# One transformer block on one core: an earlier transpose in the hand-over to the feed forward, a sum on another engine, and one block product moved up

## The chip, the cores and the metric

The kernel runs on one core of one Trainium2 chip. The metric is the device time of one launch in microseconds (us). Times of before: a median of 1028.2 us over 3 runs, from 1026.87 to 1029.06.

Five engines matter. TensorE (PE) multiplies matrices into eight banks of PSUM, VectorE (DVE) and ScalarE (ACT) read these banks and work on SBUF, GpSimd (POOL) does small powers and issues DMAs that add to what lies in SBUF, and SyncE (SP) issues the weight loads.

## The reference

One block over 512 tokens of 1024 features, in float32: a gated input projection, a convolution branch, a state-space branch, an output projection with a residual, and a gated feed forward with a second residual. The change lies between the last two.

```python
mixed = (g_conv * conv_out + g_ssm * ssm_out) @ w_out[i]
x = x + rms_norm(mixed, mix_post_g[i])
h = rms_norm(x, ffn_pre_g[i])
gt, up = jnp.split(h @ w_gate_up[i], 2, axis=-1)
f = (jax.nn.silu(gt) * up) @ w_down[i]
x = x + rms_norm(f, ffn_post_g[i])
```

## The kernel before

**Precision.** Each float32 operand is split into a high and a low half of a shorter type, and each product is three matmuls (`mm3`: high with high, and the two mixed ones). "hi" and "lo" in the names are these halves. ACT rounds the high half, DVE subtracts it from the source for the low one. For some weights the low half is made by ACT (minus the high half) and an adding DMA from POOL's queue.

**Output projection.** Tokens come in four blocks t = 0 to 3 of 128. `tm_step(ps, t, k, ...)` does step k (of eight) of block t: two column halves of 512, three matmuls each, so six matmuls 512 wide. A list `steps` gives the order; the blocks 2 and 3 are done one after the other, k from 0 to 7. When a block's last step is done, `residual(t, ps)` reads its two banks: ACT squares them and sums, DVE multiplies them by the gain, POOL takes the power -1/2 in `factor`, DVE adds to the residual rows, and the same is done again for the second norm. What comes out is the new row block xr and a diagonal matrix dg of norm factors.

**Hand-over.** `transposed(t)` turns xr into feature-major order with 16 matmuls 128 wide against dg (tile ptr), which scales it too. DVE reads the first half of the result (xg0) and ACT the second (xg1), and both make the halves of the moving operands of the feed forward: b11 and b21 from even blocks; b22, t1, t2, t3, t4 once the odd block is there as well. `mark["hi"]` and `mark["lo"]` name the last halves issued. Blocks 2 and 3 make the second half of the tokens' columns, so that the first product of the feed forward, on b11, waits for block 2.

**Feed forward.** The up and gate projections are done in units u = 0 to 21 with a scheme that needs seven block products instead of eight: `first(u)` (two products, a11 with b11 into X[u] and a12 with b21 into Y[u]), `x2`, `v1`, `x3`, `v2`, `x4`. Each `product` is twelve matmuls 256 wide (four, times three). x2, x3 and x4 add on in X[u]: ACT copies X[u] out after `first` (noted c) and after x2, DVE adds it after x3 (noted x3), and x4 closes it. The order of the units 0 to 3 is written by hand (`start`); from unit 4 on it is first(u), x4(u-1), x2(u), v2(u-1), v1(u), x3(u).

The weights of a unit are prepared by `prep_a` (a11, a12) and `prep_s`: sums s1 = a21 + a22, s3 = a11 + a21, s2 = s1 + a11, s4 = s2 + a12, and their halves (`halve`). For the units in `ADD_S1`, s1 is made by two DMAs on POOL's queue, the second of which adds; otherwise by one DVE addition. Units 0 to 3 have their sums prepared early; unit 4's is in `ADD_S1`.

**What sets the order.** A planner orders each engine's instructions when the kernel is built, by the order in the source and its own costs. `not_before(a, b)` makes it place `a` behind `b` on an engine without a wait in the run; `tc.issue_after` does so for a group; `ORDER_DVE` and `ORDER_ACT` are chains of such edges over noted instructions (lo_s2_4 is the low half of s2 of unit 4). After the units' start `mark["chain"]` keeps all products in source order.

Of the kernel before, what the change touches and what calls it, by code (L numbers as in the profile page):

```python
# [22 lines left out]
NK = D // P  # L23
# [36 lines left out]
for _n, _c in PRM:  # L60
# [22 lines left out]
TAPS_GLU = 12  # L83
TAPS = (6, 14, 18, 20, 20, 20, 20, 20)
TAPS_GATE = 5
ADD_S1 = (3, 4, 5)
ORDER_DVE = (
# [3 lines left out]
).split()  # L91
ORDER_ACT = (
    "xg1 t1h t2h c0 b22h v1_0 t3h t4h hi_s2_1 x2_0 c1 hi_s3_1 v1_1 c2 c3 x2_1 hi_s2_2 hi_s1_2 si2_0 si3_0 hi_s3_2 hi_s2_4 c4 hi_s1_4 hi_s3_4 hi_s1_5"
# [47 lines left out]
def block_kernel(ctx: ExitStack, tc: tile.TileContext, x, xT, x0, prm, hp, gp, w, out):  # L141
# [12 lines left out]
    raws, split, more_raw = {}, {}, []  # L154
# [39 lines left out]
    mark = {}  # L194
# [6 lines left out]
    def not_before(ins, first):  # L201

        edge = mybir.DependencyInfo(mybir.DependencyClass.NoSync, mybir.DependencyReason.DATA)
        tc.add_manual_dep(ins.ins, first.ins.name, edge, reason="spread")

    def mm3(ps, lh, ll, rh, rl, start, stop, more=False):

        mark["pe"] = pe.matmul(ps, lh, rh, start=start, stop=False, skip_group_check=more)  # L208
        pe.matmul(ps, lh, rl, start=False, stop=False, skip_group_check=more)  # L209
        mark["pe3"] = pe.matmul(ps, ll, rh, start=False, stop=stop, skip_group_check=more)  # L210
        return mark["pe"]
# [78 lines left out]
    ps = aux_tile("warm_ps")  # L290
# [52 lines left out]
    for k in range(1, NK):  # L343
        sq = va_tile(f"sq{k}")
# [157 lines left out]
    for j in range(NK):  # L502
# [6 lines left out]
        if j == 0:  # L509
            three = [glu_tile(n) for n in ("pv0", "pg0", "pv1")]  # L510
            ws = [w_get("val", 0), w_get("glu", 0), w_get("val", 1)]
            for k in range(NK):
                for ps, (wh, wl) in zip(three, ws):
                    c = slice(k * P, (k + 1) * P)
# [451 lines left out]
    wo0 = seq[("wo", 0)]  # L966
# [75 lines left out]
    def tm_tiles(key):  # L1042
        return [[bank(f"tm_{key}_{t}_{n}") for n in range(2)] for t in range(NT)]

    def tm_step(ps, t, k, nk, ah, al, wt, ns=(0, 1)):

        wh, wl = wt
        for n in ns:
            c = slice(n * T, (n + 1) * T)
            mm3(ps[t][n], ah, al, wh[:, c], wl[:, c], k == 0, k == nk - 1)  # L1050

    def mean_sq(src, pool_, tag, n):
        ss = sm.tile([P, 1], F32, tag=f"ss{n}", bufs=2, name=f"ss{n}_{tag}")
# [134 lines left out]
    def residual(t, ps):  # L1188

        nonlocal hold  # L1190
        xr = pbp.tile([P, D], F32, tag="xr", name=f"xr{t}")
        nc.scalar.dma_start(xr, x[t * P : (t + 1) * P, :])
        mg = pbp.tile([P, D], F32, tag="mg", bufs=1, name=f"mg{t}")
        ss = []
        for n, c in enumerate(cols2):
            ss.append(mean_sq(ps[n], pbp, f"a{t}", n))
            m = dve.tensor_tensor(out=mg[:, c], in0=ps[n], in1=gpost0[:, c], op=ALU.mult)
        if t == 3:
            hold += [mark["sq"], m]
        rs = factor(ss, f"a{t}")  # L1200
        ss = []
        for n, c in enumerate(cols2):
            dve.scalar_tensor_tensor(out=xr[:, c], in0=mg[:, c], scalar=rs, in1=xr[:, c], op0=ALU.mult, op1=ALU.add)
            ss.append(mean_sq(xr[:, c], pbp, f"b{t}", n))
        rs = factor(ss, f"b{t}")
        dg = pbp.tile([P, P], F32, tag="dg", name=f"dg{t}")
        mark["dg"] = dve.tensor_scalar(out=dg, in0=ident, scalar1=rs, scalar2=None, op0=ALU.mult)
        mark[f"dg{t}"] = mark["dg"]
        xrs[t] = xr, dg
        nc.scalar.dma_start(x2d[t * P : (t + 1) * P, :], xr)  # L1210

    def transposed(t):

        tok = slice((t // 2) * P, (t // 2 + 1) * P)
        xr, dg = xrs[t]
        xg = []
        for n in range(2):
            pt = bank(f"ptr{t}_{n}", 2 * (t == 1) + n).rearrange("p (k q) -> p k q", k=KB)
            for k in range(KB):
                c = slice((KB * n + k) * P, (KB * n + k + 1) * P)  # L1220
                m = pe.matmul(pt[:, k, :], xr[:, c], dg, start=True, stop=True)
                if t >= 2:
                    not_before(m, mark["pe3"])
                    mark["pe3"] = m
            tg = dict(tag=f"xg{t}{n}", bufs=1) if t % 2 == 0 else dict(tag=f"xg{n}", bufs=1)
            xg.append(pmp.tile([P, KB, P], F32, name=f"xg{t}_{n}", **tg))
            if n == 0:
                note("xg0", dve.tensor_tensor(
                    out=xg[n], in0=pt, in1=b3(prm_t[:, FPG + KB * n : FPG + KB * n + KB], P), op=ALU.mult
                ))  # L1230
            else:
                for k in range(KB):
                    note("xg1", act.activation(
                        xg[n][:, k], pt[:, k], AF.Copy, scale=prm_t[:, FPG + KB + k : FPG + KB + k + 1]
                    ))

        def halved(name, src, sign=1.0):
            hi, lo = [m[:, :, tok] for m in mov[name]]
            if sign > 0:
                h_ = act.copy(hi, src)  # L1240
                l_ = dve.tensor_tensor(out=lo, in0=src, in1=hi.bitcast(F32), op=ALU.subtract)
            else:
                h_ = act.activation(hi, src, AF.Copy, scale=-1.0)
                l_ = dve.scalar_tensor_tensor(
                    out=lo, in0=src, scalar=-1.0, in1=hi.bitcast(F32), op0=ALU.mult, op1=ALU.subtract
                )
            if name == "b22":
                not_before(h_, mark["hi"])
                not_before(l_, mark["lo"])
            mark["hi"], mark["lo"] = mark[name] = note(name + "h", h_), note(name + "l", l_)  # L1250

        if t % 2 == 0:
            halved("b11", xg[0])
            halved("b21", xg[1])
            xgs[t] = xg
            return
        b11, b21 = xgs[t - 1]
        t1, t2 = [pmp.tile([P, KB, P], F32, tag=f"t{i}", bufs=1, name=f"t{i}_{t}") for i in (1, 2)]

        def sums():  # L1260
            note("t1", dve.tensor_tensor(out=t1, in0=b11, in1=xg[0], op=ALU.subtract))
            note("t2", dve.tensor_tensor(out=t2, in0=t1, in1=xg[1], op=ALU.add))
            halved("t1", t1)
            halved("t2", t2, -1.0)

        def rest():
            halved("b22", xg[1])
            note("t3", dve.tensor_tensor(out=t1, in0=xg[1], in1=xg[0], op=ALU.subtract))
            halved("t3", t1)
            note("t4", dve.tensor_tensor(out=t2, in0=t2, in1=b21, op=ALU.subtract))  # L1270
            halved("t4", t2)

        return sums, rest
# [4 lines left out]
    ps = tm_tiles("wo")  # L1278
    steps = [(t, k) for k in range(4) for t in (0, 1)] + [(t, k) for t in (0, 1) for k in range(4, NK)]
    steps += [(t, k) for t in (2, 3) for k in range(NK)]  # L1280
    for t, k in steps:
        (mh, ml), tok = mt[t // 2], slice(t % 2 * P, (t % 2 + 1) * P)
        tm_step(ps, t, k, NK, mh[:, k, tok], ml[:, k, tok], split[wo0 + k])
        if k == NK - 1:
            residual(t, ps[t])
            if t == 2:
                others()
        if (t, k) == (2, 1):
            transposed(0)
            first_room = [mp.tile([P, 2, 1024], F32R, tag=f"m0{p}", name=f"a01{p}") for p in "hl"]  # L1290
            for u in range(2):
                prep_a(u, [m[:, u] for m in first_room])
        if (t, k) == (2, 5):
            sums, others = transposed(1)
            sums()
        if (t, k) in ((3, 1), (3, 2)):
            prep_a(k + 1)
        if (t, k) == (3, 4):
            halves = prep_s(0)
        if (t, k) == (3, 5):  # L1300
            with tc.issue_after(mark["pe"].ins):
                transposed(2)

    sg = {}
    c1, c2 = slice(0, HB), slice(HB, T)
# [65 lines left out]
    def x3(u):  # L1371
        f, e = u // 2, u % 2
        d = D_[u][1][:, c2]
        product(X[u], u, "s3", "t3", False)
        note(f"x3_{u}", add(d, X[u]))
        if e == 0:
            note(f"si3_{u}", act.activation(d, d, AF.Silu, scale=-1.0))
        else:
            note(f"g3_{u}", gated_by(d, d, sg[f][1][:, c2]))
# [11 lines left out]
    def x4(u):  # L1391
        f, e = u // 2, u % 2
        d = D_[u][1][:, c1]
        product(X[u], u, "a22", "t4", False)
        if e == 0:
            act.activation(d, X[u], AF.Silu, scale=-1.0)
        else:
            note(f"g4_{u}", gated_by(d, X[u], sg[f][1][:, c1]))
# [94 lines left out]
    for u in range(NF):  # L1493
        last = u == NF - 1
        if u in start:
            for n in start[u].split():
                step[n[0]](int(n[1:]))
        else:
            first(u)
            if last:  # L1500
                prep(STEPS[1])
                prep(STEPS[2])
            x4(u - 1)
            x2(u)
            if last:
                prep(STEPS[3])
            v2(u - 1)
            v1(u)
            if last:
                prep(STEPS[4])  # L1510
            x3(u)
        prep_s(max(u + 1, 3))
        prep_a(max(u + 2, 4) if u else 3)
        if u == NF - 2:
            prep(STEPS[0])
# [188 lines left out]
```

## Time and profile before

| | before |
|---|---|
| timed runs, median of 3 | 1028.2 us (1026.87 to 1029.06) |
| the profiled execution's own time | 1023.46 us |
| its span, first to last instruction | 1021.7 us |
| PE busy | 1010.2 us (99%), 6181 matmuls |
| DVE busy | 842.3 us (82%) |
| ACT busy | 616.2 us (60%) |
| POOL busy | 107.3 us (11%) |

In lines of the order of time the first number is the start in us from the span's start, the second the duration; in brackets at the end stands how long the engine had idled and what released it. L12 is line 12 of the kernel before. Matmuls are pipelined: a line's duration is longer than the distance to the next one, and it is the distance that counts.

### The profile page before, as it was taken

To read this page: it belongs to the slowest core of one execution; us is meant where nothing else is said; L and a number is where in the kernel's file an instruction comes from. 1 tells how busy PE (TensorE), PEld (TensorE's weight loads), DVE (VectorE), ACT (ScalarE), POOL (GpSimd) and SP (SyncE) were. 2 spreads that over 40 slices of the span, in tenths; PEclk is the share of its full clock that TensorE was granted. 3 is DMA by queue.
4 is the path that set the end of the run, shared out by engine and by line. 5 is a ranking of instruction groups with operands and counts; after the bars stand their busy time and mean duration, and the time that the engine had idled before them with its cause. 6 is when DMAs were issued, how large, how long until landed. Compare 5 with 4: busy or idle time off the path is not lost. (4 is left out here: it accounts for less than half of the span.)

```text
span 1021.7 us, 15952 instructions
## 1 busy us (share of the span) xinstructions
PE 1010.2 (99%) x6181; PEld 882.4 (86%) x6181; DVE 842.3 (82%) x1226; ACT 616.2 (60%) x1034; POOL 107.3 (11%) x133
## 2 busy tenths in 40 slices
PE   9999999999999999999999999999999999999997
PEld 7898889888888888888888889889999999988885
DVE  7899977968595879588987789678899887799974
ACT  7655775667656656673452676466676565678542
POOL 0101102110121012101110110011100000002000
PEclk9999999999999999999999999999999999999999
DMA  8567635645464465456352465644756355469622
GB/s 299 151 161 226 158 94 144 186 108 163 142 163 116 120 179 148 112 153 150 79 144 70 117 187 124 227 109 119 227 146 196 113 152 159 124 190 296 195 83 82
DMA packets 44459, 156.07 MB, mean 153 GB/s; under 512 B 5152, under 2 KB 6176, under 8 KB 43360
## 3 DMA queue, kind: packets, MB, share of 16 engines
q1 hardware_dynamic: 30672, 104.66, 30.4%
q0 software_dynamic: 11504, 44.05, 22.0%
q10 hardware_dynamic: 2208, 6.36, 1.9%
q8 instruction: 48, 0.79, 0.3%
q14 instruction: 27, 0.22, 0.1%
HBM read 150.78 MB, written 4.26 MB: 152 GB/s over the span
## 5 line engine op out<-in xcount | busy, mean ns | idle before, releaser
L466 DVE SCALAR_TENSOR_TENSOR a<-v,prm_t,a 128x511 f32<-128x511 f32 (+15 forms) x240 | 180.7, 756 | 15.8 <-ACT a L463 13.8
L168 ACT CAST whi<-raw 128x1024 fp32r<-128x1024 f32 (+2 forms) x108 | 106.7, 1000 | 130.6 <-PE pso L209 37.5
L175 DVE TENSOR_TENSOR wlo<-raw,whi 128x1024 fp32r<-128x1024 f32 (+2 forms) x67 | 74.9, 1124 | 37.4 <-ACT whi L168 36.6
L173 POOL DMA_DIRECT2D wlo<-in_w x41 | 36.6, 892 | 377.3 <-ACT wlo L172 112.8
L209 PE MATMUL pz<-wlo,hhi 128*128 128x512 f32 (+2 forms) x160 | 56.2, 351 | 0.3 <-DVE wlo L175 0.3
L210 PE MATMUL pz<-whi,hlo 128*128 128x512 f32 (+2 forms) x160 | 56.3, 352 | 0.0
L208 PE MATMUL pz<-whi,hhi 128*128 128x512 f32 (+2 forms) x160 | 55.4, 353 | 0.0
L208 PE MATMUL px<-hhi,whi 128*128 128x512 f32 x128 | 50.2, 392 | 0.0
L208 PE MATMUL pso<-yh,whi 128*128 128x512 f32 x128 | 50.0, 393 | 0.0
L210 PE MATMUL px<-hhi,wlo 128*128 128x512 f32 x128 | 49.8, 389 | 0.0
L209 PE MATMUL px<-hlo,whi 128*128 128x512 f32 x128 | 49.8, 389 | 0.0
L209 PE MATMUL pso<-yl,whi 128*128 128x512 f32 x128 | 49.7, 390 | 0.0
L210 PE MATMUL pso<-yh,wlo 128*128 128x512 f32 x128 | 49.7, 389 | 0.0
L1119 ACT CAST whi_g<-raw 128x1024 fp32r<-128x1024 f32 x40 | 41.2, 1052 | 12.7 <-DVE raw L1158 7.4
L550 DVE SCALAR_TENSOR_TENSOR x<-px,prm_t,x 128x511 f32<-128x511 f32 (+2 forms) x48 | 34.7, 741 | 14.3 <-ACT x L548 14.3
L1124 DVE TENSOR_TENSOR wlo_g<-raw,whi_g 128x1024 fp32r<-128x1024 f32 x34 | 41.1, 1218 | 3.8 <-ACT whi_g L1119 3.7
L172 ACT ACTIVATE wlo<-whi 128x1024 fp32r<-128x1024 f32 x41 | 43.3, 1056 | 0.3
L448 ACT ACTIVATE L<-L,nacs 128x128 f32<-128x128 f32 x128 | 38.8, 389 | 0.1
L209 PEld LDWEIGHTS pz<-wlo,hhi 128*128 128x128 f32 x160 | 30.2, 188 | 4.7 <-DVE wlo L175 0.9
L208 PEld LDWEIGHTS pz<-whi,hhi 128*128 128x128 f32 x160 | 30.2, 188 | 3.9
L210 PEld LDWEIGHTS pz<-whi,hlo 128*128 128x128 f32 x160 | 30.2, 188 | 3.7
L1119 ACT CAST chi_g<-raw 128x1024 fp32r<-128x1024 f32 x24 | 24.9, 1055 | 12.5 <-DVE raw L1158 5.9
(749 smaller groups left out, 3442.6 us busy)
## 6 DMA issues: line engine op xcount, KB each, us to landing
raw<-in_w SPq DMA_DIRECT2D x182, 512.0 KB, 4.4
wlo<-in_w POOLq DMA_DIRECT2D x41, 512.0 KB, 6.6
L<-scr POOLq DMA_DIRECT2D x8, 1024.0 KB, 7.0
wlo_g<-in_w POOLq DMA_DIRECT2D x11, 512.0 KB, 6.6
clo_g<-in_w POOLq DMA_DIRECT2D x7, 512.0 KB, 5.6
pws<-in_w POOLq DMA_DIRECT2D x8, 256.0 KB, 6.0
pw_raws<-in_w SPq DMA_DIRECT2D x4, 512.0 KB, 6.3
xr<-in_x ACTq DMA_DIRECT2D x4, 512.0 KB, 4.2
```

The source lines that it names most:

```text
L168: act.copy(hi[:, c], src[:, c])
L172: act.activation(lo[:, c], hi[:, c].bitcast(F32), AF.Copy, scale=-1.0)
L173: mark["lo"] = pool.dma_start(lo[:, c], w[n][:, c].bitcast(F32R), accum_op=ALU.add)
L175: mark["wlo"] = dve.tensor_tensor(out=lo[:, c], in0=src[:, c], in1=hi[:, c].bitcast(F32), op=ALU.subtract)
L208: mark["pe"] = pe.matmul(ps, lh, rh, start=start, stop=False, skip_group_check=more)
L209: pe.matmul(ps, lh, rl, start=False, stop=False, skip_group_check=more)
L210: mark["pe3"] = pe.matmul(ps, ll, rh, start=False, stop=stop, skip_group_check=more)
L448: act.activation(L[:, h, c, :], L[:, h, c, :], AF.Exp, bias=nacs[:, c, HG * g + h : HG * g + h + 1])
L466: return dve.scalar_tensor_tensor(out=va[j][:, d:], in0=vs[j][:, : T - d], scalar=col("dw_w", j * KC + KC - 1 - d), in1=va[j][:, d:], op0= ...
L550: dve.scalar_tensor_tensor(out=a[:, d:], in0=ps[:, : T - d], scalar=col("ssm_w", i * KS + KS - 1 - d), in1=a[:, d:], op0=ALU.mult, op1=ALU ...
L1119: a_ = act.copy(hi, src)
L1124: d_ = dve.tensor_tensor(out=lo, in0=src, in1=hi.bitcast(F32), op=ALU.subtract)
```

## The change

Four edits. First, `transposed(2)` is called behind step (3,4) instead of (3,5), and step (3,5) gets an edge behind its last matmul (`behind=spread`). Second, in `residual(3)` ACT's squares are put behind `mark["hi"]` and DVE's products behind `mark["lo"]`, which are the halves of b21 of block 2 at that point. Third, unit 4 leaves `ADD_S1`: its s1 is one DVE addition, placed in `ORDER_DVE` ahead of s3_4. Fourth, x4(5) stands directly behind x3(5) instead of behind first(6) (`ROLL = 5`).

```diff
@@ -83,11 +83,12 @@
-ADD_S1 = (3, 4, 5)
+ROLL = 5
+ADD_S1 = (3, 5)
 ORDER_DVE = (
...
-    "s3_4 s2_4 v2_2 x3_3 s4_4 lo_s2_4 lo_s1_4 s3_5"
+    "s1_4 s3_4 s2_4 v2_2 x3_3 s4_4 lo_s2_4 lo_s1_4 s3_5"
 ).split()
@@ -1042,12 +1043,14 @@
-    def tm_step(ps, t, k, nk, ah, al, wt, ns=(0, 1)):
+    def tm_step(ps, t, k, nk, ah, al, wt, ns=(0, 1), behind=None):
 
         wh, wl = wt
         for n in ns:
             c = slice(n * T, (n + 1) * T)
-            mm3(ps[t][n], ah, al, wh[:, c], wl[:, c], k == 0, k == nk - 1)
+            m = mm3(ps[t][n], ah, al, wh[:, c], wl[:, c], k == 0, k == nk - 1)
+            if behind is not None:
+                not_before(m, behind)
@@ -1195,6 +1198,9 @@
             ss.append(mean_sq(ps[n], pbp, f"a{t}", n))
             m = dve.tensor_tensor(out=mg[:, c], in0=ps[n], in1=gpost0[:, c], op=ALU.mult)
+            if t == 3:
+                not_before(mark["sq"], mark["hi"])
+                not_before(m, mark["lo"])
@@ -1280,7 +1286,8 @@
-        tm_step(ps, t, k, NK, mh[:, k, tok], ml[:, k, tok], split[wo0 + k])
+        behind = spread if (t, k) == (3, 5) else None
+        tm_step(ps, t, k, NK, mh[:, k, tok], ml[:, k, tok], split[wo0 + k], behind=behind)
@@ -1297,9 +1304,9 @@
         if (t, k) == (3, 4):
             halves = prep_s(0)
-        if (t, k) == (3, 5):
             with tc.issue_after(mark["pe"].ins):
                 transposed(2)
+            spread = mark["pe3"]
@@ -1500,7 +1507,8 @@
-            x4(u - 1)
+            if u - 1 != ROLL:
+                x4(u - 1)
@@ -1509,6 +1517,8 @@
             x3(u)
+            if u == ROLL:
+                x4(u)
```

## The prediction

> **What bounds the kernel now.** I read the page first, then the list of TensorE's waits, then the order of time on each engine around the two places that the diff touches.
>
> ```profile
> span 1021.7 us, 15952 instructions
> PE 1010.2 (99%) x6181; PEld 882.4 (86%) x6181; DVE 842.3 (82%) x1226; ACT 616.2 (60%) x1034; POOL 107.3 (11%) x133
> PEclk9999999999999999999999999999999999999999
> ```
> ```profile
> PE yv L208 <- ACT f L1369: 1.0, 1, 1.0
> ```
>
> TensorE (PE) is busy for 1010.2 of 1021.7 us at a full clock, so an edit that neither adds nor removes a matmul can only move PE's waits. The diff does neither. The longest wait behind the output projection, quoted here, is 1.0 us, in the last unit of the feed forward; two in the hand-over and one in the fifth unit stand in the rows of parts A and B, 0.3 to 0.4 each. That is 2.1 us of idle time, and each costs a little more, because a waiting matmul comes late and the next one comes 0.11 later still. So what is to be had is small, and every new wait costs its full length.
>
> **Part A: the hand-over.** Transposes of block 2 move ahead of step (3,5) of the output projection, step (3,5) is put behind them, and the squares and products of block 3's residual are put behind the halves that the transposes feed.
>
> ```profile
> 677.82 0.39 PE L210 MATMUL tm_wo<-whi,m1l 128*128 128x512 f32 x1
> ...
> 683.94 0.39 PE L210 MATMUL tm_wo<-chi,m1l 128*128 128x512 f32 x1
> ...
> 687.34 0.39 PE L210 MATMUL tm_wo<-whi,m1l 128*128 128x512 f32 x1
> 687.57 1.95 PE L1221 MATMUL ptr<-dg,xr 128*128 128x128 f32 x16
> 689.27 0.48 PE L208 MATMUL tm_wo<-whi,m1h 128*128 128x512 f32 x1
> ...
> 690.05 0.38 PE L208 MATMUL xy<-b11h,a01h 128*128 128x256 f32 x1
> 690.78 0.39 PE L209 MATMUL xy<-b11l,a01h 128*128 128x256 f32 x1 [0.34 <-DVE b11l L1241]
> ...
> 693.00 0.38 PE L209 MATMUL xy<-b21l,a01h 128*128 128x256 f32 x1 [0.43 <-DVE b21l L1241]
> ...
> 700.06 1.95 PE L1221 MATMUL ptr<-dg,xr 128*128 128x128 f32 x16
> ```
> ```profile
> 685.22 0.29 DVE L1207 TENSOR_SCALAR dg<-ident,rs_b 128x128 f32<-128x128 f32 x1 [0.75 <-POOL rs_b L1063]
> ...
> 690.03 0.69 DVE L1241 TENSOR_TENSOR b11l<-xg,b11h 128x512 fp32r<-128x512 f32 x1
> ...
> 699.12 0.29 DVE L1207 TENSOR_SCALAR dg<-ident,rs_b 128x128 f32<-128x128 f32 x1 [0.44 <-POOL rs_b L1063]
> ```
>
> Matmuls 512 wide are 0.227 apart (42 from 677.82 to 687.34). The output projection does six for each step, so the row at 683.94 is the last of step (3,4) (three are left after the transposes, fifteen lie between), and today the transposes stand in the middle of step (3,7). In the new order they would be due at 683.94 + 0.23 = 684.17. They need the diagonal dg of block 2, which is complete at 685.22 + 0.29 = 685.51; a matmul starts 0.06 after the VectorE (DVE) work it waits for (b11l ends 690.72, matmul 690.78), so they start at 685.57. **New wait: 1.4 us.** Nothing covers it: PE has only (3,5) to (3,7) left before the transposes' results, and these are held behind them.
>
> After it, the transposes take 689.27 - 687.57 = 1.70, and eighteen matmuls take 18 x 0.227, with 0.1 for the first one's late start: first unit at 691.45, against 690.05 now.
>
> What goes: from 690.05 to 700.06 PE does 72 matmuls 256 wide. They need 8.16 to 8.47 us (0.1133 or 0.1177 each, see the table under cadence), so 1.5 to 1.8 us are waits on b11l and b21l. In the new order DVE and ScalarE (ACT) get the transposes' results 2 us earlier (685.57 instead of 687.57), so b21l, which ends at 692.95 today, is complete near 690.9 with no square in between, and PE asks for it after 691.45: both waits go. The second transposes are then due at 691.45 + 8.16 to 8.47 = 699.6 to 699.9, against 700.06.
>
> What is late next is block 3's diagonal, at 699.41 today. Its chain now starts 1.4 us later at the matmuls, but today its second square starts only at 690.92, behind four ACT scalings, and a product waits for it:
>
> ```profile
> 690.92 0.61 ACT L1055 ACTIVATE jk_a<-tm_wo 128x512 bf16<-128x512 f32 x1
> ```
>
> After the change the last projection matmul starts at 691.45 - 0.23 = 691.22 and ends 0.39 later, so that square starts at 691.6, 0.7 later; b21l's 0.6 on DVE, which lies between the products and the factor today, has gone. So the diagonal is ready at about 699.5, just before PE. **Part A: -0.3 us**, between -0.5 and +0.9 (if one more split of 1.2 us is planned into the chain).
>
> The longest wait of today, 1.0 us of idle time in the last unit, leaves the clock where it was (all slices of PEclk are at 9 or more); the new one is of that size. The Trainium skill ("TensorE: Matmul & The Clock Gate", "Why this matters for your kernels") says that PE drops to half its clock after about 3 us of idleness. By that rule a wait of 1.4 us costs no more than itself, and one twice as long would cost several us; no run here shows a gap that long.
>
> **Part B: the fifth unit's sum on DVE.** s1 of unit 4 was two accumulating DMAs on GpSimd's (POOL's) queue.
>
> ```profile
> 717.86 0.56 POOL L1149 DMA_DIRECT2D s<-in_w  x1 [11.84 <-DVE dlo L1124]
> 722.18 0.86 POOL L1150 DMA_DIRECT2D s<-in_w  x1 [3.76 <-DMA s<-in_w]
> ```
> ```profile
> 729.47 0.69 DVE L1157 TENSOR_TENSOR raw<-s,raw 128x512 f32<-128x512 f32 x1 [1.91 <-DMA s<-in_w]
> ...
> 732.60 1.23 DVE L1124 TENSOR_TENSOR clo_g<-raw,chi_g 128x1024 fp32r<-128x1024 f32 x1 [0.83 <-ACT chi_g L1119]
> ```
> ```profile
> 733.26 0.28 PE L209 MATMUL xy<-t2l,chi_g 128*128 128x256 f32 x1
> 733.88 0.38 PE L210 MATMUL xy<-t2h,clo_g 128*128 128x256 f32 x1 [0.35 <-DVE clo_g L1124]
> ```
>
> DVE idles 1.91 us for that DMA, then runs s2, s4 and the split on which PE waits: 733.88 - 733.26 - 0.11 = 0.51 late, and 0.11 for the next matmul, 0.62. The sum is 0.60 on DVE (two such sums follow each other at 749.25 and 749.85 below) and goes into the idle 1.91, so s2 comes 1.3 earlier and PE's wait of 0.5 goes. **Part B: -0.6 us**; at worst -0, if the idle time on DVE has been used up and the sum only delays what follows. The other queued DMA pair, unit 5's, no longer stands behind this one on POOL's queue, which can only bring it earlier.
>
> **Part C: the sixth unit.** Block product x4(5) accumulates into the same bank from which DVE adds x3(5), so it has to wait for that add. Today two products of unit 6 lie between.
>
> ```profile
> 749.16 0.28 PE L210 MATMUL xy<-t3h,wlo_g 128*128 128x256 f32 x1
> 749.28 0.28 PE L208 MATMUL xy<-b11h,whi_g 128*128 128x256 f32 x1
> ```
> ```profile
> 749.25 0.68 DVE L1152 TENSOR_TENSOR s<-raw 128x512 f32<-128x512 f32 x1
> 749.85 0.68 DVE L1157 TENSOR_TENSOR raw<-s,raw 128x512 f32<-128x512 f32 x1
> 750.45 0.41 DVE L1308 TENSOR_TENSOR f<-xy,f 128x256 f32<-128x256 f32 x1
> ```
> ```profile
> 905.10 0.41 DVE L1308 TENSOR_TENSOR f<-xy,f 128x256 f32<-128x256 f32 x1
> ```
> ```profile
> 905.57 0.38 PE L208 MATMUL xy<-t4h,whi_g 128*128 128x256 f32 x1
> ```
>
> x3(5)'s last matmul ends at 749.44. With DVE free at once, its add starts there; the last unit's pair (add 905.10, x4 at 905.57) shows 0.47 from the add's start to x4, so x4 starts at 749.91 instead of 749.28: 0.63, with the next matmul's lateness 0.74. With DVE as it is today, the add starts at 750.45: x4 at 750.92, 1.64, with lateness 1.75. I take 1.2: DVE runs 1.3 us earlier here because of part B, but it has weight sums queued all the time and its order is fixed when the program is built. **Part C: +1.2 us**, 0.7 to 1.8.
>
> Behind it, x2(6) follows unit 6's first two products directly, so ACT's copy of X(6) has one product (1.36) of cover instead of two.
>
> ```profile
> 743.30 0.35 ACT L1319 COPY f<-xy 128x256 f32<-128x256 f32 x1
> ...
> 751.37 0.36 ACT L1319 COPY sg<-xy 128x256 f32<-128x256 f32 x1
> ```
> ```profile
> 743.71 0.39 PE L208 MATMUL xy<-t2h,whi_g 128*128 128x256 f32 x1
> ```
>
> Unit 6's first product ends at 750.52 + 0.28 = 750.80 and its copy at 751.73, 0.93 later: inside one product, so I count nothing. Unit 5's copy, at 743.30, came 2.3 us after its product and held x2(5) (743.71) by 0.17; at that lateness the bound is 1.3. Unit 5's own 0.17 should go with part B.
>
> **The sum.** -0.3 - 0.6 - 0.2 + 1.2 = +0.1 us, on the profiled execution's 1023.46 us (span 1021.7 and 1.76 around it). The three timed runs (1026.87 to 1029.06) have a median of 1028.2, 4.7 above that execution, so I carry the difference over: 1028.3.
>
> **Cadence.** PE has two speeds at the same clock, seen in the table of stretches (PE's busy time, its matmuls, the clock):
>
> ```profile
> 735.00:743.00 8.00, 8.00 (x70) 1.00 0.40 127
> 745.00:765.00 20.00, 20.00 (x179) 1.00 0.60 175
> 769.00:781.00 12.00, 12.00 (x104) 1.00 0.66 189
> 783.00:893.00 110.00, 110.00 (x973) 1.00 0.50 141
> ```
>
> Two matmuls of each count began before the stretch: 8.00 / 68 and 12.00 / 102 give 0.1177, 20.00 / 177 and 110.00 / 971 give 0.1130 to 0.1133; a product of twelve takes 1.41 or 1.36 us. The slow stretch from 735 follows the wait at 733.88, and the fast one from 745 follows the wait at 743.71. A wait thus draws the speed of what follows, up to the next break. The Trainium skill ("TensorE: Matmul & The Clock Gate", "Back-to-back issue gap") has one spacing for a width at full clock, 109 ns at 256 columns: by it there would be no second speed and no rival (1). The trace disagrees with it, 113 and 118 ns.
>
> **Rivals.** (1) *Slower: the wait before x4(5) leaves PE at 0.118.* It decides from about 40 products on (40 x 0.05 = 2.0), and the last two stretches of the table show that PE can go 110 us without a break. From 752 to 893 there are 141 / 1.36 = 104 products; half of them give 52 x 0.054 = 2.8, so 1028.3 + 2.8 = 1031.1, all of them 5.6. For it: of the two waits above one ended slow. Against: the slow stretch from 769 was over by 783. 0.20. (2) *Slower: lateness adds up* (block 3's diagonal +0.9, x4(5) +1.8, X(6) +1.3, with part B kept): +0.9 + 1.8 + 1.3 - 0.6 = +3.4, 1031.6. For it: DVE's rows from 749.25 to 750.45 follow each other without a gap. 0.10. (3) *Faster: the waits are taken promptly and the cadence ends fast*: part A -0.5, B and unit 5's wait -0.8, x4(5) +0.7, the two slow stretches of the table at the fast speed (170 x 0.0045 = 0.8) and the last unit's 1.0 gone through another order behind unit 5: -0.5 - 0.8 + 0.7 - 0.8 - 1.0 = -2.4, 1025.8. For it: the runs' median lies 4.7 above the profiled execution, which is 4.7 / 0.054 = 87 products at the slow speed, so those runs may hold more slow stretches to lose. Against: it needs all of these. 0.25. (4) *The forecast*, within 0.2% (2 us, about what a measurement of this kernel tells from no change): 0.45.
>
> Range: 1024.8 to 1031.6, which holds all four cases' values, with 1.0 below (3), since the difference between runs may bring more than the table's two stretches, and leaves out the rest of (1)'s tail. The forecast's own range goes from the sum of the low ends (-0.5 - 0.6 - 0.2 + 0.7 = -0.6, 1027.6) to where it stops being the same (+2.0, 1030.2). Faster 0.25, same 0.45, slower 0.30.
>
> **What would show it.** Right: PE idle for about 1.4 us before the block-2 transposes and none at b11l and b21l; no POOL loads for unit 4's s1 and no wait on clo_g near 733; a new wait of 0.7 to 1.8 on the first x4 matmul near 750, released by DVE's add. Wrong: block-3 transposes waiting for dg, x2(6) waiting for ACT, or PE's 256-wide spacing differing over tens of us between the two profiles; any of these over 2 us breaks the forecast.

## The result and the profile after

| | before | after |
|---|---|---|
| median of 5 | 1028.05 us (1026.87 to 1029.06) | 1022.61 us (1022.13 to 1025.12) |
| ratio after / before | | 0.9957, 95% interval 0.9943 to 0.9971 |
| profiled execution, own time | 1023.46 us | 1022.63 us |
| its span | 1021.7 us | 1020.9 us |

The changed kernel is faster by 0.43% (5.4 us), outside the forecast range. The two profiled executions differ by only 0.8 us. The page of the changed kernel:

```profile
span 1020.9 us, 15946 instructions
PE 1007.8 (99%) x6181; PEld 881.9 (86%) x6181; DVE 843.7 (83%) x1227; ACT 616.6 (60%) x1034; POOL 105.6 (10%) x131
PEclk9999999999999999999999999999999999999999
```

PE has the same 6181 matmuls, the same full clock, and 2.4 us less busy time. A PE line's busy time reaches from one matmul into the next, so fewer busy microseconds for the same matmuls mean that more of them stand closer together. The list of PE's waits (us in total, times, longest), of after:

```profile
PE xy L209 <- DVE f L1315: 1.3, 1, 1.3
PE ptr L1227 <- issue: 1.3, 1, 1.3
...
PE yv L209 <- ACT f L1376: 0.2, 1, 0.2
```

Two new waits of 1.3 us are there, the ones that the prediction priced: block 2's transposes (ptr) and x4 of unit 5 (xy, L209). The waits on b11l, b21l and clo_g are gone, and the last unit's wait on ACT has shrunk from 1.0 to 0.2. (One of 0.9 in the first 25 us, between the rows shown, lies where nothing was edited.) In the order of time, PE at the hand-over and at x4(5), and DVE at x4(5):

```profile
684.39 0.39 PE L211 MATMUL tm_wo<-chi,m1l 128*128 128x512 f32 x1
686.05 2.02 PE L1227 MATMUL ptr<-dg,xr 128*128 128x128 f32 x16 [1.27 <-issue]
...
700.52 1.95 PE L1227 MATMUL ptr<-dg,xr 128*128 128x128 f32 x16
...
748.73 0.28 PE L211 MATMUL xy<-t3h,wlo_g 128*128 128x256 f32 x1
750.29 0.39 PE L209 MATMUL xy<-t4h,whi_g 128*128 128x256 f32 x1 [1.28 <-DVE f L1315]
```
```profile
748.62 0.68 DVE L1155 TENSOR_TENSOR s<-raw 128x512 f32<-128x512 f32 x1
749.22 0.68 DVE L1160 TENSOR_TENSOR raw<-s,raw 128x512 f32<-128x512 f32 x1
749.82 0.42 DVE L1315 TENSOR_TENSOR f<-xy,f 128x256 f32<-128x256 f32 x1
```

The hand-over, from the last matmul of step (3,4) to block 3's transposes, takes 700.52 - 684.39 = 16.13 us; it took 700.06 - 683.94 = 16.12. x4(5) starts 1.56 behind x3(5)'s last matmul, where the next matmul of before, the first one of unit 6, starts 0.12 behind it; the add that x4(5) waits for stands behind two weight sums on DVE. So by its instructions the change costs about what the prediction said. The 5.4 us must be somewhere that neither list shows.

**Where they are.** One more profile of the unchanged kernel, of an execution of 1026.98 us (span 1025.2), which is nearer to its median than the first one, shows it. The table of stretches has the stretch, its length, PE's busy time with its matmuls, the granted clock, the DMA share and GB/s. First the kernel before in its first profiled execution (1023.46), then in the second one (1026.98), then after:

```profile
704.00:740.00 36.00, 35.65 (x313) 1.00 0.65 184
752.00:815.00 63.00, 63.00 (x553) 1.00 0.54 159
820.00:900.00 80.00, 80.00 (x707) 1.00 0.49 141
```
```profile
704.00:740.00 36.00, 36.00 (x308) 1.00 0.64 183
752.00:815.00 63.00, 63.00 (x538) 1.00 0.55 152
820.00:900.00 80.00, 80.00 (x681) 1.00 0.51 145
```
```profile
704.00:740.00 36.00, 36.00 (x320) 1.00 0.60 176
752.00:815.00 63.00, 63.00 (x558) 1.00 0.54 159
820.00:900.00 80.00, 80.00 (x708) 1.00 0.50 143
```

But for one wait of 0.35 us in the first row, all say that PE is busy without a gap at a clock of 1.00, and yet the same 80 us hold 681 or 708 matmuls: 80 / 679 = 0.1178 us apart or 80 / 706 = 0.1133 (two of each count began before the stretch). In its second profile the kernel before runs at 0.118 from 701 us to the last unit's end; in its first, behind 701, it did so only for 10 and 14 us. Its wait list has nothing on clo_g and nothing on ACT's f. It begins so, and the two rows behind these lie ahead of the output projection:

```profile
PE warm_ps L292 <- DVE woken L287: 1.0, 1, 1.0
PE xy L209 <- DVE b21l L1241: 0.4, 1, 0.4
PE xy L209 <- DVE b11l L1241: 0.3, 1, 0.3
```

With PE slower, DVE and ACT keep ahead here, and the waits of the quick execution behind 701 us are not there. From here on, the *short* and the *long* spacing are 0.113 and 0.118.

The difference between this execution and after's can be followed by the same matmul in both: last of step (3,4), first behind block 3's transposes, x3(5)'s last, the next product's first (that is x4(5) after), and the last of the last unit's y product.

```profile
683.56 0.39 PE L210 MATMUL tm_wo<-chi,m1l 128*128 128x512 f32 x1
...
701.12 0.36 PE L208 MATMUL xy<-b11h,whi_g 128*128 128x256 f32 x1
...
749.14 0.28 PE L210 MATMUL xy<-t3h,wlo_g 128*128 128x256 f32 x1
749.26 0.28 PE L208 MATMUL xy<-b11h,whi_g 128*128 128x256 f32 x1
...
908.81 0.28 PE L210 MATMUL yv<-b22h,wlo_g 128*128 128x256 f32 x1
```
```profile
702.22 0.37 PE L209 MATMUL xy<-b11h,whi_g 128*128 128x256 f32 x1
...
904.46 0.28 PE L211 MATMUL yv<-b22h,wlo_g 128*128 128x256 f32 x1
```

After minus before: +0.83, +1.10, -0.41, +1.03, -4.35. The +0.83 arose ahead of the first edit and goes with the execution: experiment 9's profile of the changed kernel has the row of 684.39 at 683.39. So the hand-over gives +0.27, the rest of units 0 to 5 gives -1.51 (short spacing in most of it), x4(5) +1.44, and everything behind it -5.38. The own times differ by 1022.63 - 1026.98 = -4.35. Nearly all of the gain lies behind the place where the change adds its longest wait to the feed forward.

### The profile page after: what moved, and what is told of

It is laid out like the page before. It is cut to its first block, busy times and chain, and to the rows that moved or that the text cites. A ratio compares the mean times of both kernels' runs of the same rounds, so it can differ in the third digit from the quotient of the medians.

```text
span 1020.9 us, 15946 instructions
## 1 busy us (share of the span) xinstructions
PE 1007.8 (99%) x6181; PEld 881.9 (86%) x6181; DVE 843.7 (83%) x1227; ACT 616.6 (60%) x1034; POOL 105.6 (10%) x131
## 4 chain that ended last, share of the span: by engine, by line
PE 88%; DVE 6%; ACT 2%; issue 1%; DMA 1%; SPq 0%; POOL 0%; ACTq 0%; DVEq 0%; POOLq 0%
PE xy L209 4%; PE xy L211 4%; PE xy L210 4%; PE pso L209 3%; PE pso L210 3%; PE pso L211 3%; PE pz L210 3%; PE pz L211 3%; PE px L211 2%; PE px L209 2%; PE px L210 2%; PE pz L209 2%; PE yv L209 2%; PE yv L210 2%; PE yv L211 2%
## 5 line engine op out<-in xcount | busy, mean ns | idle before, releaser
L209 PE MATMUL pz<-whi,hhi 128*128 128x512 f32 (+2 forms) x160 | 55.4, 353 | 0.0
L209 PE MATMUL px<-hhi,whi 128*128 128x512 f32 x128 | 50.2, 392 | 0.0
L209 PE MATMUL pso<-yh,whi 128*128 128x512 f32 x128 | 50.0, 393 | 0.0
L209 PEld LDWEIGHTS pz<-whi,hhi 128*128 128x128 f32 x160 | 30.2, 189 | 3.8
```

## The experiments

All times are medians with their range and number; the ratio is to the kernel before as timed beside the experiment, and it lies near the ratio of the means, which with two groups of times isn't that of the medians. The experiments were timed in four sets (1 to 4, 5 to 8, 9 to 12, 13 and 14), each on another chip. With these and the table above the kernel before ran 119 times, and its times lie in two groups: 25 under 1025 us, most others between 1026 and 1029; the granted clock is 0.997 to 0.999 in both. So beside each median stands how many lay under 1025.

**1. The kernel before again.** No edit.

> The kernel before, unchanged. Question: what do its ordinary executions (1026.9 to 1029.1) hold that its profiled one (1023.46) did not? Theory C (cadence): a long slow stretch (0.118 instead of 0.113 per 256-wide matmul) in the feed forward, above all in units 8 to 20: 971 matmuls x 0.0044 = 4.3 us. Theory W (waits): a longer wait in unit 4, whose sum waits for an accumulating DMA that can land later: a wait of about 5 us instead of 0.5. If this run's profile is of an execution near 1028, C shows slow spacing between 783 and 893 with the waits as before, W a long wait on clo_g near 733.

1026.87 us (1021.48 to 1028.74, 12; 3 under 1025), ratio 0.9991 (0.9975 to 1.0007). Its profile is the one above: the median execution of before is one with the long spacing from 701 us on, and the execution that I predicted from was one of the rarer quick ones.

**2. The hand-over alone** (edits one and two).

```diff
         if (t, k) == (3, 4):
             halves = prep_s(0)
-        if (t, k) == (3, 5):
             with tc.issue_after(mark["pe"].ins):
                 transposed(2)
+            spread = mark["pe3"]
...
+            if t == 3:
+                not_before(mark["sq"], mark["hi"])
+                not_before(m, mark["lo"])
```

> Edits 1 and 2 alone (earlier transposes, residual of block 3 behind them). By the sum of the waits: 0 to -0.3 us, 1028. Theory C: no change of what follows unit 4's wait, 1028 +- 1; if the spacing behind the hand-over changes, up to 0.3. Theory W: 1028.

1024.64 us (1021.94 to 1028.03, 12; 6 under 1025), ratio 0.9991 (0.9970 to 1.0011): not told from before. The profiled execution (1025.97) has the short spacing from 701 to 779.6 and the long one from a wait there (0.19 us of idleness) to the end.

**3. Unit 4's sum on DVE alone** (edit three).

```diff
-ADD_S1 = (3, 4, 5)
+ADD_S1 = (3, 5)
...
-    "s3_4 s2_4 v2_2 x3_3 s4_4 lo_s2_4 lo_s1_4 s3_5"
+    "s1_4 s3_4 s2_4 v2_2 x3_3 s4_4 lo_s2_4 lo_s1_4 s3_5"
```

> Edit 3 alone (unit 4's sum on VectorE). By the sum of waits: -0.8, 1027.2. Theory C: as much as that, unless the removed waits at 733 and 743 change which speed follows; then up to -5 (1023) or none. Theory W: all of the gain, 1022.6 to 1023.5.

1026.73 us (1021.19 to 1028.09, 12; 1 under 1025), ratio 1.0001 (0.9985 to 1.0017). The wait on clo_g that it takes away is not there in the usual execution, so there is nothing to win.

**4. x4(5) behind x3(5) alone** (edit four).

```diff
+ROLL = 5
...
-            x4(u - 1)
+            if u - 1 != ROLL:
+                x4(u - 1)
...
+            if u == ROLL:
+                x4(u)
```

> Edit 4 alone (x4 of unit 5 directly behind x3). By the sum of waits: +1.2 to +1.8, 1029.5. Theory C: the new wait draws a new speed: the gain is here if it ends fast and nothing breaks it (1028 + 1.5 - 4.5 = 1025), otherwise 1029.5. Theory W: 1029.5.

1023.51 us (1022.61 to 1025.54, 11; 10 under 1025), ratio 0.9972 (0.9957 to 0.9986). The one edit that only adds a wait is the only one of the three that is faster by itself. PE at that wait, and the table of stretches:

```profile
749.60 0.28 PE L211 MATMUL xy<-t3h,wlo_g 128*128 128x256 f32 x1
750.71 0.39 PE L209 MATMUL xy<-t4h,whi_g 128*128 128x256 f32 x1 [0.83 <-DVE f L1309]
```
```profile
704.00:740.00 36.00, 36.00 (x308) 1.00 0.64 186
...
820.00:900.00 80.00, 80.00 (x709) 1.00 0.50 144
```

308 matmuls in 36 us ahead of the wait, as in the second profile of before; 709 in 80 us behind it, as in after. PE comes to the wait with the long spacing and leaves it with the short one.

**5. The change without edit four.**

```diff
-ROLL = 5
...
-            if u - 1 != ROLL:
-                x4(u - 1)
+            x4(u - 1)
...
-            if u == ROLL:
-                x4(u)
```

> The changed kernel without edit 4 (edits 1 to 3 alone). The runs so far: the kernel before takes either about 1022 or about 1027, and its trace at 1026.98 runs at 0.118 us per 256-wide matmul from 701 to 905. Theory C (cadence; the wait before x4(5) puts the slow stretch back to fast): without that wait the two groups of times come back, 1021 to 1022 and 1026 to 1027, with fewer in the slow one than before, as in e2. Rival S (sum: the edits' own savings add up): all runs at 1022 to 1023.

1025.91 us (1021.12 to 1029.0, 12; 4 under 1025), ratio 0.9999 (0.9977 to 1.0021). Without the fourth edit the gain is gone. In its profile the short spacing of 701 to 742 is lost at a break of 0.09 us, where the first matmul of x2(5) has 0.20 to the next:

```profile
742.55 0.36 PE L208 MATMUL xy<-t2h,whi_g 128*128 128x256 f32 x1
742.75 0.28 PE L209 MATMUL xy<-t2l,whi_g 128*128 128x256 f32 x1
```
```profile
704.00:740.00 36.00, 36.00 (x320) 1.00 0.59 173
...
820.00:900.00 80.00, 80.00 (x682) 1.00 0.50 143
```

**6. The wait seven units later.** The kernel before with edit four at unit 12 (`ROLL = 12`), so that it comes near 818 us instead of 750. If it is the wait that ends the long spacing, less of it is left to save.

> The kernel before with edit 4 at unit 12 instead of 5, near 817 instead of 749. Theory C: runs that are slow from 701 stay so for 68 us longer than in e4, 68/1.41 = 48 products x 0.054 = 2.6 us more than e4: 1026; runs that are fast take 1022 + 1. Rival P (place: it is the order of unit 5 and 6, a weight buffer or a bank that comes free earlier): no gain, 1027 + 1.

1026.01 us (1024.01 to 1027.46, 12; 1 under 1025), ratio 1.0008 (0.9992 to 1.0024).

```profile
817.87 0.28 PE L211 MATMUL xy<-t3h,clo_g 128*128 128x256 f32 x1
818.78 0.39 PE L209 MATMUL xy<-t4h,chi_g 128*128 128x256 f32 x1 [0.64 <-DVE sg L1309]
```
```profile
752.00:815.00 63.00, 63.00 (x537) 1.00 0.54 154
820.00:900.00 80.00, 80.00 (x707) 1.00 0.50 145
```

537 matmuls in 63 us ahead of the wait (long), 707 in 80 behind it (short). The switch moved with the wait, and the time went up with it, from 1023.5 to 1026.0 (two sets, in which the kernel before had 1027.25 and 1027.03): 68 us more at the long spacing are 68 x 0.0045 / 0.118 = 2.6 us.

**7. A break without a wait.** The kernel before with one small matmul that nothing holds up, ahead of unit 6's first product; its result is overwritten.

```diff
+        if u == 6:
+            last = mark["pe3"]
+            mark["pe3"] = pe.matmul(xy[:, HB : HB + 64], ident, ident[:, :64], start=True, stop=True)
+            not_before(mark["pe3"], last)
```

> The kernel before with one more matmul, 64 wide with operands that are ready, ahead of unit 6's first product; products in the old order, no wait. It is left over work and changes no result. Theory C in its strong form (any break in the stream of like matmuls draws the speed anew): 1023 to 1024 in most runs. Theory C in its weak form (it takes idle time of PE): 1027 as before. Rival P: 1027.

1022.73 us (1020.53 to 1028.06, 12; 8 under 1025), ratio 0.9987 (0.9964 to 1.0010). Eight of twelve are quick, where the kernel before had 12 of 35 in the same set. The execution that was profiled (1027.86) is one of the other four: long spacing ahead of the break and behind it. So a break of the stream without idle time seems to change the spacing in some executions and not in others; the profile shows only one in which it didn't, and the median's ratio doesn't tell it from before.

**8. The same matmul made to wait** for x3(5)'s output (`d[:, :64]` in place of `ident[:, :64]`).

> The same as e7, but the 64-wide matmul reads what VectorE's x3 add of unit 5 writes, so that PE waits 0.6 to 1.6 us, and the products stay in the old order. Theory C: as e4, 1023 to 1024.5 in all runs. Rival P (the order of products): 1027 + 1.

1026.86 us (1025.64 to 1033.11, 12; 0 under 1025), ratio 1.0032 (1.0009 to 1.0054). The wait came out longer than I had meant, since this output is also gated on DVE (L1407) behind another split:

```profile
749.08 0.28 PE L210 MATMUL xy<-t3h,wlo_g 128*128 128x256 f32 x1
751.65 0.43 PE L1333 MATMUL xy<-f,ident 128*128 128x64 f32 x2 [2.29 <-DVE f L1407]
```
```profile
749.00:752.00 3.00, 0.70 (x7) 1.00 0.64 126
752.00:757.00 5.00, 5.00 (x31) 0.66 0.66 210
757.00:765.00 8.00, 8.00 (x73) 1.00 0.44 133
```

After 2.29 us of idleness the granted clock is 0.66 from 752 to 757 us, a stretch in which 31 matmuls run, where experiment 13 has 46; then the spacing is short (73 in 8 us). In this execution (1026.31) 2.5 us of wait (751.65 - 749.08 - 0.12) and 15 x 0.113 = 1.7 us of lost clock eat much of what the short spacing brings. It is the one experiment whose interval lies above 1, and that comes from other executions: seven executions take 1025.6 to 1026.9 us, five 1029.8 to 1033.1, at like granted clocks (0.996 to 0.999 and 0.995 to 0.998). None of the five was profiled. An estimate: some 1300 matmuls behind the wait at the long spacing instead of the short one are 1300 x 0.0045 = 5.9 us, which is about the distance of the two groups. So in these PE may have left the wait with the long spacing; that is argued, not shown.

**9. The change again.** No edit to it.

> The changed kernel, unchanged, beside its variants. Theory C: one group of times, 1022 to 1023.5, none near 1027, since the wait before x4(5) leaves PE fast each time. If a few lie near 1027, the wait only often does so.

1023.22 us (1021.64 to 1023.94, 5; 5 under 1025), ratio 0.9958 (0.9946 to 0.9970). Together with the table above 9 of 10 lie under 1025. Its profile (1021.64) is the quickest of the sixteen: PE comes to x4(5) with the short spacing, waits 1.47 us and leaves with the short one.

```profile
747.55 0.28 PE L211 MATMUL xy<-t3h,wlo_g 128*128 128x256 f32 x1
749.29 0.39 PE L209 MATMUL xy<-t4h,whi_g 128*128 128x256 f32 x1 [1.47 <-DVE f L1315]
```

**10. The change with x3(5)'s add ahead of the weight sums**, which makes the wait shorter.

```diff
-    "s1_4 s3_4 s2_4 v2_2 x3_3 s4_4 lo_s2_4 lo_s1_4 s3_5"
+    "s1_4 s3_4 s2_4 v2_2 x3_3 s4_4 lo_s2_4 lo_s1_4 s3_5 s3_7 x3_5 s1_8 s2_7 lo_s2_6"
```

> The changed kernel with VectorE's x3 add of unit 5 planned ahead of two weight sums, about 0.6 us earlier; the wait before x4(5) falls from 1.45 to about 0.85. Theory C: the shorter wait resets the speed as well: 1022.0, one group. Rival L (the reset needs a long wait): two groups, 1022 and 1026 to 1027.

1023.18 us (1022.02 to 1027.67, 10; 7 under 1025), ratio 0.9972 (0.9957 to 0.9988). The profiled execution (1026.66) is one of the three others:

```profile
747.89 0.28 PE L211 MATMUL xy<-t3h,wlo_g 128*128 128x256 f32 x1
749.12 0.39 PE L209 MATMUL xy<-t4h,whi_g 128*128 128x256 f32 x1 [0.96 <-DVE f L1315]
```
```profile
704.00:740.00 36.00, 36.00 (x320) 1.00 0.58 172
...
820.00:900.00 80.00, 80.00 (x682) 1.00 0.50 145
```

Here the same kind of wait does the opposite: short ahead of it (320 in 36 us), long behind it (682 in 80). A wait does not end the long spacing as such; it can begin it, if PE arrives with the short one.

**11. The change without edit four, but with unit 5's copy earlier on ACT**, so that x2(5) isn't late.

```diff
-    ... hi_s1_4 hi_s3_4 hi_s1_5"
+    ... hi_s1_4 hi_s3_4 hi_s1_5 hi_s3_5 c5 hi_a11_6"
```

> Edits 1 to 3 without edit 4, and ScalarE's copy of X(5) planned one split earlier, so that x2(5) does not come 0.09 us late at 743. In the trace of e5 that short break is where PE went from 0.113 to 0.118 for the rest. Theory C: without it PE stays fast to the next break: the slow group shrinks or goes, 1021 to 1022 in most runs. If another short break follows (x3 of unit 7 at 767 came late in the kernel before), the slow group stays.

1022.32 us (1020.5 to 1028.26, 12; 9 under 1025), ratio 0.9969 (0.9949 to 0.9988). So there is a second way to a gain of about this size, without any wait at x4(5). What it does in its quick executions I can't show: the one that was profiled (1028.26) has the long spacing from 701 to the end. That the short spacing, once had, now meets no break near 743 fits, but is only argued.

**12. The change with both orders** (10 and 11).

> The changed kernel with both: the add of unit 5 earlier and the copy of X(5) earlier, so that PE comes to the wait before x4(5) in its fast state. Theory C, if a wait of this kind ends fast from either state: 1021.5, one group. If a wait flips the state, as the block of transposes does in the traces so far (fast to slow six times, slow to fast four times): 1026 to 1027 in most runs.

1024.01 us (1021.72 to 1030.2, 12; 7 under 1025), ratio 0.9977 (0.9960 to 0.9994). The profiled execution (1028.11) is like that of experiment 10: short spacing up to the wait of 1.07 us at x4(5), long from there.

**13. The change with x3(5)'s add later**, which makes the wait longer.

```diff
-    "s1_4 s3_4 s2_4 v2_2 x3_3 s4_4 lo_s2_4 lo_s1_4 s3_5"
+    "s1_4 s3_4 s2_4 v2_2 x3_3 s4_4 lo_s2_4 lo_s1_4 s3_5 s2_7 lo_s1_7 x3_5 lo_s2_6"
```

> The changed kernel with VectorE's x3 add of unit 5 planned 0.6 us later, behind one more weight split: the wait before x4(5) grows from 1.45 to about 2.0. Theory L (the longer the wait, the surer the fast speed behind it): one group, 1023.2, none over 1025. Theory R (the wait only redraws, and the drawn share is chance): two groups as in e10, 1023 and 1027. A wait of 2.3 us of idle time in e8 had the clock granted at 0.66 for the next 5 us; if that happens here, 1025 to 1026.

1024.3 us (1023.04 to 1028.66, 12; 10 under 1025), ratio 0.9975 (0.9963 to 0.9988). In its profile PE idles 1.89 us, arrives long and leaves short, and the clock stays at 1.00 behind it:

```profile
750.11 0.38 PE L209 MATMUL xy<-t4h,whi_g 128*128 128x256 f32 x1 [1.89 <-DVE f L1315]
```
```profile
750.00:757.00 7.00, 6.89 (x60) 1.00 0.49 155
752.00:757.00 5.00, 5.00 (x46) 1.00 0.67 213
```

**14. The change with unit 5's copy earlier**, so that PE comes to the wait at x4(5) without the break near 743. The edit is that of experiment 11 on the whole change.

> The changed kernel with ScalarE's copy of X(5) one split earlier, and the wait before x4(5) as it is: PE comes to the wait fast, or as the transposes left it. Theory L: one group, 1021.5 to 1022.5, and a version that is faster than the changed kernel by 0.1 (no late x2(5)) to 0.5. Theory R, or a wait that flips a fast state: two groups, 1022 and 1027, as in e12.

1022.76 us (1021.99 to 1024.38, 5; 5 under 1025), ratio 0.9956 (0.9943 to 0.9968): not told from the change itself (0.9957, 0.9958). Its profile has the long spacing from 701 to 749.8, a wait of 0.83 us of idleness at x4(5), and the short one behind it. So it doesn't show what follows when PE comes there short, which the experiment was for. None of the fourteen beats the change by more than can be told.

**All breaks together.** In the sixteen profiled executions I took every place between 703 and 898 us where two matmuls of 256 columns start more than 0.126 us apart, and the spacing ahead of it and behind it (the half-clock stretch of experiment 8 counts as part of its wait). There are 26. Of the 9 that PE reached with the long spacing, 8 ended short (the ninth is experiment 7's). Of the 17 that it reached with the short one, 9 ended long and 8 short. Between breaks the spacing stayed as it was, for up to 200 us. Block 3's transposes near 700 are a break too: all 6 executions that came to them short left long (experiments 1, 3, 4, 6, 7 and 8), and of the 10 that came long 8 left short. With the hand-over's edits PE came to them long in all 9 profiles, and it left short in 7 of these, against 1 of the 7 without; that is where the -1.51 comes from. By itself it doesn't last: in experiments 2 and 5 a later break ended it.

The profiles fit this account: with the short spacing PE catches up with its feeders and meets small breaks, about half of which put it on the long one; with the long spacing it meets hardly any (besides the x4 waits and the matmuls added by experiments 7 and 8 two, both in the first profile of before), and mostly stays there to the last unit. The wait at x4(5) is 0.8 to 1.5 us long, so it is met at either spacing, and in the profiles it took PE off the long one each time. Not shown is why a break sets one spacing or the other: waits of 0.83 and 1.89 us ended short, those of 0.96 and 1.07 long, and these two groups also differ in the spacing on arrival; one of 1.47 that was met short ended short (experiment 9). Nor is the effect shown to belong to waits: experiment 7 adds none and has eight quick executions of twelve, and experiment 8's slow ones may have left a wait long.

## Why the prediction was wrong

**Part A, the hand-over: mechanism right, gain not there.** The new wait was priced at 1.4 us and measures 686.05 - 684.39 - 0.23 = 1.43. The waits on b11l and b21l went, and nothing waits for block 3's diagonal. The stretch came out even (16.13 against 16.12) where -0.3 was forecast. About half of this is that all 72 matmuls ran at the long spacing, the upper end of the 8.16 to 8.47 that I had allowed; the rest is that the first of them came 692.04 - 684.39 = 7.65 behind step (3,4), not 7.51.

**Part B, unit 4's sum: right against the execution that I had, worth nothing in the usual one.** Between the two first profiles the wait on clo_g goes, as priced. But experiment 3, with that edit alone, has a ratio of 1.0001: the second profile of before, at the long spacing, doesn't have that wait, and experiment 2's, which has the sum as before and the short spacing at that place, doesn't either.

**Part C, x4(5): size right.** 1.2 us was taken, 0.7 to 1.8 allowed; the start moved from 0.12 behind x3(5)'s last matmul to 1.56, and with the 0.11 by which the next one is late, as the prediction counts it, that is 1.55, by the add's place behind two weight sums on DVE, as at the range's upper end. x2(6) didn't wait for ACT.

**The step that failed is the sum's last line**, "so I carry the difference over: 1028.3". I took the 4.7 us between the profiled execution and the median as something that both kernels have alike. The second profile of before, 3.5 us above the first, shows what it is: the long spacing from 701 us to the last unit's end, which the first profiled execution happened not to have. Against this usual execution the change saves 5.38 us behind x4(5), more than the 4.35 by which the two executions differ in all. The edit that looked like the whole cost, part C, is what takes this spacing away: experiment 4 against experiment 5 shows it from both sides, and experiment 6 moves it. The prediction's own signs of being wrong had named this one, PE's spacing "differing over tens of us between the two profiles"; it took the second profile of before to see it.

**Rival 1 had the mechanism with the wrong sign.** It let the wait at x4(5) leave PE at 0.118 for the rest of the run, from a profile in which PE comes to that place at 0.113. In the usual execution of before it comes at 0.118, and then the wait ended short in every profile in which it was an x4 wait (after and experiments 4, 6, 13 and 14). Arriving short it ended long in two profiles of three (10 and 12, against 9), so rival 1 does happen. In the change itself it can only be rare: 1 of 10 executions lies above 1025, at 1025.12, and it wasn't profiled.

**Rival 3 named the cause and then didn't price it.** It had "those runs may hold more slow stretches to lose" and 87 products for the 4.7 us, which is about what was lost; but its sum took only the 0.8 us of the two slow stretches in the one profile. With the whole 4.7 in place of that 0.8, its -2.4 would have been -6.3, and with part C at its measured cost about -5.5; the runs gave -5.4. That the two agree so well is in part chance, since part B's gain and the last unit's 1.0 aren't there in the usual execution. The likeliest case should have been split by which execution is the usual one, since the gap between profile and median was on the page.

**The cadence section held.** 0.1177 and 0.1133 are the spacings between breaks in all sixteen profiles, but for a few us of lower clock in experiment 8; nearly the whole gain is a change from one to the other at a clock of 1.00. The Trainium skill ("TensorE: Matmul & The Clock Gate", "Back-to-back issue gap") has one figure for 256 columns at full clock, 262 cycles, about 109 ns, and calls it the gap of an isolated matmul. It has no second one; the traces here have two, 113 and 118 ns.

## What to carry to other kernels

When the profiled execution is quicker than the median by more than the change can be worth, profile the kernel again until you have the usual execution, and predict from that one: waits seen in a quick execution may not exist in the usual one. In a kernel that is bound by PE, compare the number of matmuls in equal stretches, since busy share and granted clock can be the same while the spacing differs by 4%. A wait in a stream that has none is not only its length; here one of about a microsecond, placed early, bought back five, while one of 2.5 us at the same place (experiment 8) bought nothing.

## What the runs showed of the hardware

- PE has two stable spacings for this stream of 256-column matmuls at the same granted clock of 1.00: 0.1133 and 0.1178 us. In the profiles one lasts until a break, up to 200 us, and of 26 breaks 17 changed it.
- 2.29 us of idleness were followed by a granted clock of 0.66 from 752 to 757 us (experiment 8, PE back at 751.65), while 1.89 us left it at 1.00 (experiment 13). Each is one execution. The Trainium skill ("TensorE: Matmul & The Clock Gate", "Why this matters for your kernels") puts the point at about 3 us. In the one run here with a gap that long the loss came earlier, and the measurement decides.
- Behind block 3's 16 transposes of 128 columns the spacing is not the one ahead of them in 14 of 16 profiles.
